# Second mixer: ada sums traced behind a head's maxima, none between heads and out-projection; last feed-forward: prepared weights ahead of the first convolutions

## The chip, the cores and the metric

The kernel runs on one core of a Trainium2 chip. The metric is the device time of one execution in microseconds. The core's engines work side by side, each through its own instructions in order, and wait for one another through semaphores: TensorE (PE; its weight loads are listed as PEld) multiplies matrices, VectorE (DVE) and ScalarE (ACT) do elementwise work and read TensorE's accumulators, GpSimd (POOL) does small elementwise work, and SyncE (SP) issues the DMAs.

## The reference

One step of a two-layer diffusion backbone for two groups of 128 tokens each: a context group and a latent group, which also attends to 128 cached context keys. The model width is 2048, the feed-forward width 5632. Each layer has a mixer and a gated feed-forward, each behind an RMS norm with shift, scale and gate computed from a condition vector:

```python
mod = jax.nn.silu(cond) @ w_ada[l] + b_ada[l]
sh1, sc1, gt1, sh2, sc2, gt2 = jnp.split(mod[:, None, :], 6, axis=-1)
h = rmsnorm(x, g_norm_mix[l]) * (1 + sc1) + sh1
...
x = x + gt1 * m
h = rmsnorm(x, g_norm_ffn[l]) * (1 + sc2) + sh2
x = x + gt2 * conv_ffn(h, w_ffn_up[l], w_ffn_conv[l], b_ffn_conv[l], w_ffn_down[l])
```

The change touches the second layer. Its mixer is differential attention with eight heads of two score halves each:

```python
s = jnp.einsum("bqhjd,bkhjd->bhjqk", qb, k).astype(jnp.float32) * scale
p = jax.nn.softmax(s, axis=-1)
a = (p[:, :, 0] - lam * p[:, :, 1]).astype(v.dtype)
return jnp.einsum("bhqk,bkhd->bqhd", a, v)
...
o = rmsnorm(o, g_sub) * (1.0 - lambda_init)
return o.reshape(b, t, -1) @ w_out, new_ctx
```

Its feed-forward multiplies by w_ffn_up, convolves each feature over three neighbouring positions, and gates:

```python
u = up[:, :-2] * w_conv[0] + up[:, 1:-1] * w_conv[1] + up[:, 2:] * w_conv[2] + b_conv
gate, val = u[..., :D_FF], u[..., D_FF:]
return (jax.nn.silu(gate) * val) @ w_down
```

## The kernel before

**Products.** Features lie on the 128 partitions, the 256 tokens of both groups along the free dimension. A product of one chunk of 128 output features runs through 16 blocks of the weights (`gemm`). Weights and activations are each split into a high part rounded to the fast format and the low remainder, so a block takes three matmuls (high x high, high x low, low x high), and a chunk 48. A weight tile of 1 MB is loaded by SP (`raw`, three buffers), ScalarE rounds it into `wh` and VectorE subtracts that into `wl` (`split`, L240 and L241; `wh` and `wl` have four buffers of half a chunk each). `Weights.ahead` does this for half a chunk before a product asks for it, `first_three` runs the first three chunks of a projection together, with the blocks of the last head (14 and 15) last.

**The order.** The program is traced in Python, and a planner then orders each engine's instructions by a simulated timeline, older ones first among those that are ready. `keep_order` (shortened to `pin` where it is optional) holds an instruction behind the one that was traced just before it on the same engine. In the heads of the second mixer every TensorE instruction is held in this way (`pe.in_turn`).

**The ada work.** The modulation of each sub-layer is computed beside the other work, in three ways. `row_step` does units of it on TensorE. The class `Deep` does six units (`DEEP`) on VectorE: 96 sums (`sums`, L553; each multiplies half a row of weights with the silu of the condition and adds up), whose weight blocks SP loads, one block of two sums at a time, into two buffers (`block`, L550); six further steps load and activate the second half of the condition, and six finish a unit: 108 steps in all. A sum's full product is thrown away into `deep.junk`, which is `o_all` (named hx in the profile) during the heads and `u` (hxc) from the out-projection on. Both the sums and their loads are held in program order. `side_pump`, called by `pump`, takes as many steps as a rate per product says: 2.2 in the heads from the second on, 1.5 in the out-projection.

**The heads.** `project(h)` makes six products per head, two chunks each of query, key and value. Half way through each product its hook `middle` calls `pump`, which advances the earlier head's attention by one stage (`step`), takes side steps, and does a row step; in the last product the hook then also starts this head's `attend`. Its first stage is scores, row maxima (`softmax_parts`, L850 and L851), the negated maxima on GpSimd (L853), exponentials on ScalarE (L858), reciprocals and the combination of the two halves (L1231 to L1237). Later stages transpose the values (`evs`, copied by ScalarE at L1216), transpose and apply the weights, normalise (squares L1260, factor on GpSimd L1264 and L1266, product L1268), transpose back and split the output into `o_all`. After the eighth head `flush` traces its remaining stages.

**The out-projection** follows: `first_three`, then six steps of `Deep` (`AHEAD`), then a loop over 16 chunks with residual (L826), the prepared rows of the next norm (`raw_rows`, L680 and L683) and `pump`.

**The last feed-forward.** `modulated` hands over products already made (`ready`): three in the first layer, four in the second, where no ada unit is left for TensorE, and one further chunk of prepared weights. `conv` takes them one by one: ScalarE scales (L1338), VectorE adds the two neighbours (L1341, L1344). While products are ready its instructions are held in order, and after the one that leaves two products, and the one that leaves one, it calls `W.ahead` for half a chunk.

Of the kernel before, what the change touches and what calls it, by code (L numbers as in the profile page):

```python
# [14 lines left out]
ALU = mybir.AluOpType  # L15
AX = mybir.AxisListType
# [5 lines left out]
T = 128  # L22
# [7 lines left out]
HEAD_SCALE = 128 ** -0.5  # L30
# [23 lines left out]
PEW = {"heads": 1.0, "out0": 1.0, "c": 1.0}  # L54
QUIET = [4, 3, 3]
LATE = 3
AHEAD = 6

EARLY = (2, 5, 8, 11, 13)
WIDER = (32, 16, 8, 4, 2)  # L60
# [22 lines left out]
FLIMIT = {"ab": 0, "ffn0": 12, "c": 12, "ffn1": 16}  # L83

BESIDE = [17, 18, 19]
SIDE = {"in3": 0.6, "heads": 1.05, "out0": 0.9, "c": 2.2, "outc": 1.5}
UW = NT + 2
INV = {2048: 0, 768: 1, 512: 2, 128: 3, 256: 4}

# [2 lines left out]
def step_kernel(ctx: ExitStack, tc: tile.TileContext, A: dict):  # L92
# [419 lines left out]
    def side_pump():  # L512
        side["due"] += side["rate"]
        while side["due"] >= 1.0:
            side["due"] -= 1.0
            side_step()
            deep.step()
# [88 lines left out]
            ada["i"] += 1  # L606
            ada["t"] = 0

    def pump(rows, feats=0.0, until=None):

        until = until or RLIMIT[stage[0]]
        step()
        side_pump()
        ada["due"] += rows
        while ada["due"] >= 0.25:
            if ada["i"] >= until and not later:
                ada["due"] = 0.0
                break
            ada["due"] -= 0.25 if ada["i"] >= until else 0.25 * ada["pew"]
            row_step(until)  # L620
        feat["due"] += feats
        while feat["due"] >= 1.0 and feat["i"] < FLIMIT[stage[0]]:
            feat["due"] -= 1.0
            feature_step()
# [219 lines left out]
        dve.tensor_tensor(out=dst, in0=dst, in1=t[:, :heads], op=ALU.add)  # L844


    def softmax_parts(s, mx, sums, rs, const, p):

        nmx = T_(small, [P, 2], "nmx")
        dve.tensor_reduce(out=mx[:, 0:1], in_=s[:, 0:T], axis=AX.X, op=ALU.max)  # L850
        dve.tensor_reduce(out=mx[:, 1:2], in_=s[:, T:3 * T], axis=AX.X, op=ALU.max)  # L851
        if rs is None:
            pool.tensor_scalar(out=nmx, in0=mx, scalar1=-const, scalar2=None, op0=ALU.mult)  # L853
        else:
            pool.tensor_scalar(out=nmx, in0=mx, scalar1=-1.0, scalar2=None, op0=ALU.mult)
            pool.tensor_tensor(out=nmx, in0=nmx, in1=rs, op=ALU.mult)
        for g, c in ((0, slice(0, T)), (1, slice(T, 3 * T))):
            act.activation(p[:, c], s[:, c], AF.Exp, bias=nmx[:, g:g + 1],  # L858
                           scale=const if rs is None else rs[:, g:g + 1],
                           accum_out=sums[:, g:g + 1])  # L860
# [305 lines left out]
    def mixer_c(cp, hx, W, ready, st):  # L1166
# [4 lines left out]
        def product(rate):  # L1171

            def middle():
                pump(rate)
                while soon:
                    soon.pop(0)()
            return ready.pop(0) if ready else gemm(W.chunk(), xh, xl, between=middle)

        o_all = operand(keep, "hx")
# [38 lines left out]
        def attend(h, q, k, v, evs):  # L1218
            mx = T_(small, [P, 2, 2], "dmx")
            sums = T_(small, [P, 2, 2], "dsums")  # L1220
            pj = []
            for j in range(2):
                s = T_(ppool["att"], [P, 512], "att", bufs=3)
                for g, ks in ((0, slice(0, T)), (1, slice(T, 3 * T))):
                    pe.matmul(s[:, ks], q[:, j, g * T:(g + 1) * T], k[:, j, ks],
                              start=True, stop=True)
                p = T_(cp, [P, 3 * T], f"p{j}", bufs=1)
                softmax_parts(s, mx[:, j], sums[:, j], None, HEAD_SCALE, p)
                pj.append(p)
            rec = T_(small, [P, 2, 2], "drec")  # L1230
            dve.reciprocal(out=rec, in_=sums)  # L1231
            nl = T_(small, [P, 2], "nl")
            dve.tensor_scalar(out=nl, in0=rec[:, 1], scalar1=nlam, scalar2=None, op0=ALU.mult)
            for g, ks in ((0, slice(0, T)), (1, slice(T, 3 * T))):
                dve.tensor_scalar(out=pj[1][:, ks], in0=pj[1][:, ks], scalar1=nl[:, g:g + 1],
                                  scalar2=None, op0=ALU.mult)
                dve.scalar_tensor_tensor(out=pj[0][:, ks], in0=pj[0][:, ks],  # L1237
                                         scalar=rec[:, 0, g:g + 1], in1=pj[1][:, ks],
                                         op0=ALU.mult, op1=ALU.add)
            yield  # L1240
            pt = T_(ppool["att"], [P, 512], "att", bufs=3)
            for i in range(2):
                for g in range(2):
                    pe.transpose(pt[:, g * NT + i * P:g * NT + (i + 1) * P],
                                 evs[:, i, g * T:(g + 1) * T], ident)
            act.copy(v[:, 0], pt[:, 0:NT])
            act.copy(v[:, 2], pt[:, NT:])
            sp.dma_start(out=A["o_diff_v"][:, h], in_=v[:, 0])
            yield
            yield  # L1250
            pT = transposed(cp, pj[0])
            yield
            o = T_(ppool["att"], [P, 512], "att", bufs=3)
            pe.matmul(o[:, 0:NT], pT[:, 0:T], v[:, 0], start=True, stop=True)
            pe.matmul(o[:, NT:], pT[:, T:2 * T], v[:, 1], start=True, stop=False)
            pe.matmul(o[:, NT:], pT[:, 2 * T:], v[:, 2], start=False, stop=True)
            ss = T_(small, [P, 2], "ss")
            on = T_(cp, [P, 2, NT], "on", bufs=1)
            for g in range(2):
                act.activation(on[:, g], o[:, g * NT:(g + 1) * NT], AF.Square,  # L1260
                               accum_out=ss[:, g:g + 1])
            var = T_(small, [P, 2], "var")
            left = (1.0 - LAMBDA_INIT) ** 2
            pool.tensor_scalar(out=var, in0=ss, scalar1=1.0 / (256 * left), scalar2=EPS / left,  # L1264
                               op0=ALU.mult, op1=ALU.add)
            pool.tensor_tensor(out=var, in0=var, in1=C("mhalf")[:, 0:2], op=ALU.pow)  # L1266
            for g in range(2):
                dve.scalar_tensor_tensor(out=on[:, g], in0=o[:, g * NT:(g + 1) * NT],  # L1268
                                         scalar=var[:, g:g + 1], in1=C("gsub"),
                                         op0=ALU.mult, op1=ALU.mult)  # L1270
            yield
            yield
            pt = T_(ppool["att"], [P, 512], "att", bufs=3)
            for i in range(2):
                for g in range(2):
                    pe.transpose(pt[:, i * NT + g * T:i * NT + (g + 1) * T],
                                 on[:, g, i * P:(i + 1) * P], ident)
            src = pt.rearrange("p (i t) -> p i t", i=2)
            split(o_all[:, 2 * h:2 * h + 2, :NT], o_all[:, 2 * h:2 * h + 2, NT:2 * NT], src)
# [11 lines left out]
        oh, ol = (lambda k: o_all[:, k, :NT]), (lambda k: o_all[:, k, NT:2 * NT])  # L1291
        ready = first_three(W, oh, ol, LAST_LATE)
        side["rate"] = SIDE["outc"]
        for _ in range(AHEAD):
            deep.step()
        for c in range(KD):
            fine[0] = c >= KD - QUIET[2]
            residual(ready.pop(0) if ready else gemm(W.chunk(), oh, ol), l, 0, c, st)
# [12 lines left out]
    def ffn(hx, W, ready, turn, l, st):  # L1311
        xh, xl = (lambda k: hx[:, k, :NT]), (lambda k: hx[:, k, NT:2 * NT])
        wider = list(WIDER)

        def product():
            if ready:
                return ready.pop(0)
            if in_order:
                return gemm(W.chunk(), xh, xl, between=in_order.pop(0))
            if wider:  # L1320
                n = NT + wider.pop(0)
                return gemm(W.chunk(), xh, xl, more=lambda k: hx[:, k, :n])
            return gemm(W.chunk(), xh, xl)
# [3 lines left out]
        with tc.tile_pool(name=f"ffn{l}", bufs=1) as fp, banks(f"pffn{l}") as pf:  # L1327
# [5 lines left out]
            def conv(m):  # L1333
                early = bool(ready)
                pin = keep_order if early else lambda i: i
                ps = product()
                y = T_(fp, [P, NT], "cv", bufs=3)
                pin(act.activation(y, ps, AF.Identity, scale=cw[:, 1, m:m + 1], bias=cw[:, 3, m:m + 1]))  # L1338
                y3 = y.rearrange("p (g t) -> p g t", g=2)
                p3 = ps.rearrange("p (g t) -> p g t", g=2)  # L1340
                pin(dve.scalar_tensor_tensor(out=y3[:, :, 1:], in0=p3[:, :, :T - 1],  # L1341
                                             scalar=cw[:, 0, m:m + 1], in1=y3[:, :, 1:],
                                             op0=ALU.mult, op1=ALU.add))
                pin(dve.scalar_tensor_tensor(out=y3[:, :, :T - 1], in0=p3[:, :, 1:],  # L1344
                                             scalar=cw[:, 2, m:m + 1], in1=y3[:, :, :T - 1],
                                             op0=ALU.mult, op1=ALU.add))
                if early and 0 < len(ready) < 3:
                    W.ahead(pin)
                return y

# [233 lines left out]
```

## Time and profile before

| what | us |
|---|---|
| median of three runs (lowest, highest) | 2333.0 (2331.63, 2339.8) |
| the profiled execution's own time | 2332.29 |
| its span, first to last instruction | 2330.5 |
| TensorE busy in the span | 2287.4 |
| VectorE busy | 1873.5 |
| ScalarE busy | 1200.3 |

The stages of the second layer in the span: heads of the mixer until about 1490 us, out-projection from about 1495 to 1598, its feed-forward's first products until about 1620, the rest of that feed-forward and the final norm until the end.

How the rows read. A timeline row has the start in us from the span's beginning, the duration in us, engine, line, operation, what is written and read, how many instructions are merged, and in brackets the engine's idle time before it with what ended that. A row of the chain of waits has start, duration, and the work that the end waited for. A row of windows gives the stretch, its length, then busy time and count for each engine, the clock that TensorE was granted (1.00 is full), the DMA engines' busy share and their rate. Matmuls are pipelined, so a row's duration is longer than the distance from one to the next.

### The profile page before, as it was taken

The numbers are of one execution on the slowest core, as the hardware profiler recorded it, in microseconds if no ns is written. First come the engines' busy times: TensorE is split into PE (matmuls) and PEld (weight loads), VectorE is DVE, ScalarE is ACT, GpSimd is POOL, SyncE is SP. The second block draws the span as 40 slices with busy tenths as digits, with TensorE's granted clock in tenths as the row PEclk, the third lists the DMA queues.
The fourth block names the chain that finished last, engine by engine and source line by source line (L and its number), as shares of the span: only waits on it lengthen the run. The fifth ranks groups of instructions, "written<-read, shape, count | busy, mean of one in ns | idle before, by whom it ended". The sixth has DMA issues, their size and how long they took to land.

```text
span 2330.5 us, 47639 instructions
## 1 busy us (share of the span) xinstructions
PE 2287.4 (98%) x19544; PEld 2187.1 (94%) x19544; DVE 1873.5 (80%) x2920; ACT 1200.3 (52%) x1982; POOL 186.1 (8%) x242
## 2 busy tenths in 40 slices
PE   6999999999999999999999999999999999999998
PEld 4788778999999999999999999999999999999998
DVE  3569767889999999999978878898999965666654
ACT  4245555575553355555575454457655434555543
POOL 0002111210000000001131000014000000000011
PEclk9999999999999999999999999999999999999999
DMA  9888888687777777777788888765777755555553
GB/s 366 346 339 291 314 310 324 231 298 260 260 262 280 300 271 265 260 257 259 290 294 294 296 320 321 280 237 193 255 265 263 261 204 191 192 197 197 188 195 127
DMA packets 102170, 615.05 MB, mean 264 GB/s; under 512 B 11008, under 2 KB 19008, under 8 KB 34752
## 3 DMA queue, kind: packets, MB, share of 16 engines
q1 hardware_dynamic: 101952, 612.01, 71.9%
q8 instruction: 153, 2.51, 0.4%
q14 instruction: 65, 0.53, 0.1%
HBM read 607.22 MB, written 4.75 MB: 263 GB/s over the span
## 4 chain that ended last, share of the span: by engine, by line
PE 91%; DVE 3%; DMA 2%; ACT 1%; issue 1%; POOL 1%; SPq 0%; DVEq 0%; ACTq 0%
PE acc L107 84%; PE ada L107 3%; PE att L107 2%; DVE wl L241 1%; DMA araw<-w_ada 1%; PE att L110 1%; DMA raw<-w_in_ab 1%; ACT wh L240 1%; DMA block<-w_ada 1%; PE misc L107 0%; DVE hx L553 0%; DMA raw<-w_out_c 0%; PE ada L110 0%; POOL dev L790 0%; DVE hxc L553 0%
## 5 line engine op out<-in xcount | busy, mean ns | idle before, releaser
L107 PE MATMUL acc<-hx,wh 128*128 128x256 f32 (+1 forms) x7264 | 1259.1, 278 | 7.8 <-ACT hx L664 4.3
L240 ACT CAST wh<-raw 128x1024 fp32r<-128x1024 f32 (+2 forms) x826 | 795.3, 974 | 912.5 <-PE acc L107 726.8
L107 PEld LDWEIGHTS acc<-hx,wh 128*128 128x128 f32 x7264 | 1101.3, 189 | 38.9 <-issue 15.9
L241 DVE TENSOR_TENSOR wl<-raw,wh 128x1024 fp32r<-128x1024 f32 (+2 forms) x826 | 920.7, 1131 | 254.1 <-ACT wh L240 249.4
L107 PE MATMUL acc<-hx,wl 128*128 128x256 f32 (+1 forms) x3632 | 1007.7, 278 | 4.4 <-DVE wl L241 4.3
L107 PEld LDWEIGHTS acc<-hx,wl 128*128 128x128 f32 x3632 | 685.2, 189 | 6.9 <-DVE wl L241 6.0
L107 PE MATMUL acc<-g,wh 128*128 128x256 f32 x2816 | 478.8, 276 | 0.0
L107 PEld LDWEIGHTS acc<-g,wh 128*128 128x128 f32 x2816 | 423.6, 188 | 0.0
L107 PE MATMUL acc<-g,wl 128*128 128x256 f32 x1408 | 388.0, 276 | 0.0
L456 DVE CUSTOM_DVE_ANT_0 junk<-araw,condb 128x2048 f32<-128x2048 f32 x128 | 294.3, 2300 | 0.0
L107 PE MATMUL acc<-hxc,wh 128*128 128x256 f32 (+1 forms) x1568 | 282.3, 281 | 0.0
L107 PEld LDWEIGHTS acc<-g,wl 128*128 128x128 f32 x1408 | 264.2, 188 | 0.0
L107 PEld LDWEIGHTS acc<-hxc,wh 128*128 128x128 f32 x1568 | 241.2, 189 | 4.5 <-issue 4.2
L107 PE MATMUL acc<-hxc,wl 128*128 128x256 f32 (+1 forms) x784 | 218.2, 278 | 0.0
L203 POOL TENSOR_TENSOR sqacc<-sqacc,sq 128x256 f32<-128x256 f32 x62 | 68.5, 1104 | 1511.5 <-ACT sq L199 1505.4
L107 PEld LDWEIGHTS acc<-hxc,wl 128*128 128x128 f32 x784 | 147.5, 188 | 0.4
L553 DVE CUSTOM_DVE_ANT_0 hx<-block,condb 128x1024 fp32r<-128x1024 f32 x82 | 100.1, 1221 | 18.8 <-DMA block<-w_ada 18.3
L107 PE MATMUL ada<-araw,condw 128*32 128x512 f32 (+1 forms) x672 | 82.6, 591 | 13.7 <-DMA araw<-w_ada 13.6
L1338 ACT ACTIVATE cv<-acc,convw 128x256 f32<-128x256 f32 x169 | 94.4, 559 | 0.0
L826 DVE SCALAR_TENSOR_TENSOR x<-acc,mod,x 128x128 f32<-128x128 f32 x190 | 57.7, 345 | 39.4 <-PE acc L107 39.2
L1344 DVE SCALAR_TENSOR_TENSOR cv<-acc,convw,cv 128x254 f32<-128x254 f32 x169 | 81.0, 479 | 3.1
L1341 DVE SCALAR_TENSOR_TENSOR cv<-acc,convw,cv 128x254 f32<-128x254 f32 x169 | 80.5, 476 | 0.0
(243 smaller groups left out, 1498.7 us busy)
## 6 DMA issues: line engine op xcount, KB each, us to landing
raw<-w_up SPq DMA_DIRECT2D x176, 1024.0 KB, 4.8
araw<-w_ada SPq DMA_DIRECT2D x142, 1024.0 KB, 5.6
raw<-w_down SPq DMA_DIRECT2D x88, 1024.0 KB, 4.8
raw<-w_in_c SPq DMA_DIRECT2D x48, 1024.0 KB, 7.1
block<-w_ada SPq DMA_DIRECT2D x48, 512.0 KB, 6.7
raw<-w_in_ab SPq DMA_DIRECT2D x19, 1024.0 KB, 6.8
raw<-w_out_ab SPq DMA_DIRECT2D x16, 1024.0 KB, 7.0
raw<-w_out_c SPq DMA_DIRECT2D x16, 1024.0 KB, 5.8
```

Source lines behind the costliest of these rows:

```text
L107: return self.placed(nc.tensor.matmul(*a, **kw))
L110: return self.placed(nc.tensor.transpose(*a, **kw))
L203: eng.tensor_tensor(out=st["acc"], in0=st["acc"], in1=sq, op=ALU.add)
L240: pin(act.copy(out_hi, src))
L241: pin(dve.tensor_tensor(out=out_lo, in0=src, in1=out_hi.bitcast(F32), op=ALU.subtract))
L456: keep_order(dve.tensor_tensor_reduce(out=T_(feat["pool"], [P, D], "junk"), in1=feat["row"][:, c], in0=feat["raw"].rearrange("p g n -> p ( ...
L553: keep_order(dve.tensor_tensor_reduce(out=self.junk[:, 14:16, :512], in0=self.raw, in1=self.row[:, c].rearrange("p (g n) -> p g n", g=2), ...
L826: dve.scalar_tensor_tensor(out=x[:, c, s], in0=ps[:, s], scalar=mod[:, l, 3 * which + 2, c, g:g + 1], in1=x[:, c, s], op0=ALU.mult, op1=AL ...
L1338: pin(act.activation(y, ps, AF.Identity, scale=cw[:, 1, m:m + 1], bias=cw[:, 3, m:m + 1]))
L1341: pin(dve.scalar_tensor_tensor(out=y3[:, :, 1:], in0=p3[:, :, :T - 1], scalar=cw[:, 0, m:m + 1], in1=y3[:, :, 1:], op0=ALU.mult, op1=ALU.add))
L1344: pin(dve.scalar_tensor_tensor(out=y3[:, :, :T - 1], in0=p3[:, :, 1:], scalar=cw[:, 2, m:m + 1], in1=y3[:, :, :T - 1], op0=ALU.mult, op1=A ...
```

## The change

Five edits. `AHEAD` and its six steps of `Deep` between `first_three` and the loop go. The out-projection's rate of side steps becomes 2.0 instead of 1.5. In the heads' hook the side steps move from `pump` to the end, behind the start of a head's `attend`. The two maxima of each score half are held in program order. In the second layer's feed-forward the two calls of `W.ahead` move from behind the second and the third convolution to in front of the first and the second; `long` is true where four products are ready.

```diff
-AHEAD = 6
...
-SIDE = {"in3": 0.6, "heads": 1.05, "out0": 0.9, "c": 2.2, "outc": 1.5}
+SIDE = {"in3": 0.6, "heads": 1.05, "out0": 0.9, "c": 2.2, "outc": 2.0}
...
-    def pump(rows, feats=0.0, until=None):
+    def pump(rows, feats=0.0, until=None, beside=True):
 
         until = until or RLIMIT[stage[0]]
         step()
-        side_pump()
+        if beside:
+            side_pump()
...
-    def softmax_parts(s, mx, sums, rs, const, p):
+    def softmax_parts(s, mx, sums, rs, const, p, pin=lambda i: i):
 
         nmx = T_(small, [P, 2], "nmx")
-        dve.tensor_reduce(out=mx[:, 0:1], in_=s[:, 0:T], axis=AX.X, op=ALU.max)
-        dve.tensor_reduce(out=mx[:, 1:2], in_=s[:, T:3 * T], axis=AX.X, op=ALU.max)
+        pin(dve.tensor_reduce(out=mx[:, 0:1], in_=s[:, 0:T], axis=AX.X, op=ALU.max))
+        pin(dve.tensor_reduce(out=mx[:, 1:2], in_=s[:, T:3 * T], axis=AX.X, op=ALU.max))
...
             def middle():
-                pump(rate)
+                pump(rate, beside=False)
                 while soon:
                     soon.pop(0)()
+                side_pump()
...
-                softmax_parts(s, mx[:, j], sums[:, j], None, HEAD_SCALE, p)
+                softmax_parts(s, mx[:, j], sums[:, j], None, HEAD_SCALE, p, keep_order)
...
         side["rate"] = SIDE["outc"]
-        for _ in range(AHEAD):
-            deep.step()
         for c in range(KD):
...
     def ffn(hx, W, ready, turn, l, st):
...
+        long = len(ready) > 3
...
                 pin = keep_order if early else lambda i: i
+                if len(ready) > 4 - 2 * long:
+                    W.ahead(pin)
                 ps = product()
...
-                if early and 0 < len(ready) < 3:
+                if early and ready and not long:
                     W.ahead(pin)
                 return y
```

## The prediction

> **What bounds the kernel now.** I read the page's totals first, then the chain that ended last in order of time, then windows over the two places that the change names, then the timelines there.
>
> ```profile
> span 2330.5 us, 47639 instructions
> PE 2287.4 (98%) x19544; PEld 2187.1 (94%) x19544; DVE 1873.5 (80%) x2920; ACT 1200.3 (52%) x1982; POOL 186.1 (8%) x242
> ```
>
> TensorE is the bound nearly everywhere, so an edit on the other engines can only earn the time in which TensorE waits or runs slowly. The chain leaves TensorE for long in one late place, between the heads of the second mixer and its out-projection, and runs there through VectorE and a load of ada weights:
>
> ```profile
> 1505.17 9.32 DMA block<-w_ada
> 1514.62 1.23 DVE hxc L553
> 1515.89 1.23 DVE hxc L553
> 1517.78 9.96 PE acc L107 x65
> ```
>
> The windows give each stretch: heads, transition, the two halves of the out-projection, the start of the last feed-forward; then two short ones to compare clocks (columns: busy us and count of PE, PEld, DVE, ACT, POOL, granted clock, DMA share, GB/s).
>
> ```profile
> 1213.00:1477.00 264.00, 262.29 (x2203) 250.32 (x2202) 229.04 (x390) 141.54 (x265) 20.87 (x26) 1.00 0.85 307
> ...
> 1511.00:1523.00 12.00, 7.09 (x36) 6.29 (x35) 9.28 (x23) 4.69 (x9) 1.05 (x1) 0.72 0.27 97
> 1523.00:1560.00 37.00, 37.00 (x325) 35.44 (x324) 36.56 (x64) 20.91 (x39) 8.70 (x8) 1.00 0.77 285
> 1560.00:1598.00 38.00, 38.00 (x338) 38.00 (x336) 29.34 (x54) 21.98 (x45) 6.16 (x7) 1.00 0.57 195
> ...
> 1625.00:1632.00 7.00, 5.83 (x48) 5.38 (x47) 6.24 (x12) 6.48 (x11) 0.00 (x0) 1.00 0.76 287
> ```
> ```profile
> 1518.20:1522.40 4.20, 4.20 (x21) 4.20 (x21) 2.86 (x8) 3.34 (x8) 0.00 (x0) 0.50 0.34 122
> 1523.00:1527.00 4.00, 4.00 (x37) 4.00 (x36) 4.00 (x6) 2.78 (x7) 1.70 (x2) 1.00 0.78 262
> ```
>
> TensorE loses about 5 us of 12 in the transition, under 2 of 264 in the heads, 1.2 of 7 at the feed-forward's start, and nothing in the out-projection. What can be won is therefore some 10 us of 2330.
>
> **The transition: no sums between heads and out-projection.** What TensorE, VectorE, ScalarE and GpSimd do there, one fence each:
>
> ```profile
> 1513.30 0.85 PE L110 MATMUL att<-cst,on 128*128 128x128 f32 x4 [1.89 <-DVE on L1268]
> 1514.82 0.61 PE L107 MATMUL acc<-hx,wh 128*128 128x256 f32 x3 [0.68 <-ACT hx L240]
> 1517.78 0.58 PE L107 MATMUL acc<-hx,wh 128*128 128x256 f32 x1 [2.34 <-DVE hx L241]
> ```
> ```profile
> 1510.26 1.22 DVE L553 CUSTOM_DVE_ANT_0 hxc<-block,condb 128x1024 fp32r<-128x1024 f32 x1
> ...
> 1512.67 0.87 DVE L1268 SCALAR_TENSOR_TENSOR on<-att,var,cst 128x256 f32<-128x256 f32 x2
> 1514.62 1.23 DVE L553 CUSTOM_DVE_ANT_0 hxc<-block,condb 128x1024 fp32r<-128x1024 f32 x1 [1.07 <-DMA block<-w_ada]
> ...
> 1517.04 0.69 DVE L241 TENSOR_TENSOR hx<-att,hx 128x512 fp32r<-128x512 f32 x1
> ```
> ```profile
> 1514.19 0.59 ACT L240 CAST hx<-att 128x512 fp32r<-128x512 f32 x1 [4.36 <-PE att L110]
> ```
> ```profile
> 1479.28 0.71 POOL L1266 TENSOR_TENSOR var<-var,cst 128x2 f32<-128x2 f32 x1
> ...
> 1510.48 1.57 POOL L1266 TENSOR_TENSOR var<-var,cst 128x2 f32<-128x2 f32 x1
> ```
>
> The sums that write hxc before the out-projection are the six of AHEAD. The last head's output is late behind the last four of them, two ahead of L1268 and two ahead of the subtraction that writes hx. Without them its hi/lo subtraction starts when ScalarE's cast ends, 1514.19 + 0.59 = 1514.78, not 1517.04: 2.3 us. The norm product L1268 starts when its GpSimd factor is there, 1510.48 + 1.57 = 1512.05, not 1512.67: 0.6. The factor took 0.71 one head earlier, when no sum ran beside it, and 1.57 here beside one: 0.86, an estimate. Together 3.7 of the 4.9 us of waits (1.89 + 0.68 + 2.34). The ends are 2.9 (GpSimd no faster) and 4.9 (the head's chain also starts earlier, since its maxima no longer stand behind a sum).
>
> Behind the wait TensorE ran 21 matmuls in 4.20 us at a granted clock of 0.50; at 1.00 it runs 37 in 4.00. So 4.20 - 21 x 4.00/37 = 1.9 us are lost to the clock. With 1.2 us of waiting left I count all of that as won; the lower end is nothing, since no wait between 0.76 and 4.9 us shows me where the clock falls. The Trainium skill (TensorE: Matmul & The Clock Gate, Why this matters for your kernels) says that a gap of over about 3 us brings the half clock. The trace agrees at 4.9 us; by that rule any end of the row above leaves too short a gap, and the sum keeps 1.9, where the rows alone leave 0 to 1.9.
>
> **What that costs in the out-projection.** The six sums move behind the residuals.
>
> ```profile
> L553 DVE CUSTOM_DVE_ANT_0 hxc<-block,condb 128x1024 fp32r<-128x1024 f32 x14 | 17.6, 1257 | 1.2 <-DMA block<-w_ada 1.1
> ```
>
> Fourteen sums with this form ran: six ahead, eight in the out-projection at 1.5 steps a chunk. Afterwards all fourteen run there, at 2.0 a chunk over eight chunks: 6 x 1.257 = 7.5 us more on VectorE, and three block loads with them. From 1523 to 1560 VectorE is busy 36.56 of 37 us, and yet TensorE never waits; from 1560 on it has 38.00 - 29.34 = 8.7 us free. So the ends are 0 (all of it slides into the later room) and 7.5 (all of it stands before weight splits). The nearest row is the full VectorE without a TensorE wait, so I take a third: 2.5.
>
> **The heads: sums behind the maxima.** Two of the heads' waits are of the kind the change removes; one in full:
>
> ```profile
> 1294.68 1.22 DVE L553 CUSTOM_DVE_ANT_0 hx<-block,condb 128x1024 fp32r<-128x1024 f32 x1
> ...
> 1295.82 0.29 DVE L850 TENSOR_REDUCE dmx<-att 128x1 f32<-128x128 f32 x1
> ```
> ```profile
> 1296.78 0.37 ACT L858 ACTIVATE p<-att,nmx 128x128 f32<-128x128 f32 x1 [3.69 <-POOL nmx L853]
> ...
> 1299.95 0.38 ACT L1216 COPY dev<-acc 128x256 f32<-128x256 f32 x1
> ```
> ```profile
> 1300.39 0.44 PE L110 MATMUL att<-cst,dev 128*128 128x128 f32 x2 [0.76 <-ACT dev L1216]
> ```
> ```profile
> 1340.50 0.44 PE L110 MATMUL att<-cst,dev 128*128 128x128 f32 x2 [0.64 <-ACT dev L1216]
> ```
>
> A sum delays the maxima, the exponentials hold ScalarE 3.69 us, and the copy of the values that TensorE transposes stands behind them. With the maxima over a microsecond earlier ScalarE is free in time: 0.76 + 0.64 = 1.4, of which I take 1.2. The maxima are now held behind the VectorE instruction traced before them, the hi/lo subtraction of the head before, which TensorE has fed by then; that adds no wait. The other end is a loss. Each sum is held behind the VectorE instruction traced just before it; that was work of the step before, and is now the head's last softmax combination (L1237), which waits for both exponentials. Behind the sum stand the next sums and, on SP's queue, the block loads and what follows them there:
>
> ```profile
> 1488.21 9.87 SPq L550 DMA_DIRECT2D block<-w_ada  x2
> 1498.96 0.56 SPq L287 DMA_DIRECT2D raw<-w_out_c  x1
> ```
>
> A block load can thus stand 9.87 us, with a load of weights behind it. About two sums a head, 2.5 us, now fill the time between maxima and combination and will no longer; over seven heads that is 17.6 us, against 264.00 - 229.04 = 35 us in which VectorE is idle in this stretch. I take no loss; all 17.6 on TensorE is the far end. TensorE's order in the heads stays as traced, since the moved calls issue nothing on it there.
>
> **The last feed-forward.**
>
> ```profile
> 1624.07 1.12 ACT L240 CAST wh<-raw 128x512 fp32r<-128x512 f32 x2
> ```
> ```profile
> 1625.13 0.48 DVE L1344 SCALAR_TENSOR_TENSOR cv<-nt,convw,cv 128x254 f32<-128x254 f32 x1
> 1625.53 1.29 DVE L241 TENSOR_TENSOR wl<-raw,wh 128x512 fp32r<-128x512 f32 x2
> ```
> ```profile
> 1626.27 0.38 PE L107 MATMUL acc<-hx,wl 128*128 128x256 f32 x1 [0.53 <-DVE wl L241]
> ...
> 1630.02 0.39 PE L107 MATMUL acc<-hx,wl 128*128 128x256 f32 x1 [0.63 <-DVE wl L241]
> ```
>
> Each half tile is two casts and two subtractions (1.12 and 1.29 us the pair). They move ahead of the first and second convolution, whose two VectorE instructions of 0.48 us come later instead; their results have no reader on TensorE until the down-projection. The weight load itself is long issued in both. Both waits go, 0.53 + 0.63 = 1.2 us; VectorE is busy 6.24 of 7.00 us there, so some of it returns with the next chunk's weights: 0.9 (ends 0 and 1.2). In the first feed-forward the conditions come out as before.
>
> **Sum.** -3.7 - 1.9 + 2.5 - 1.2 - 0.9 = -5.2 us. The profiled execution took 2332.3 us with its span of 2330.5, so 2327.1; the median of the three runs is 0.7 above it, so 2327.8.
>
> **Rivals.** (1) The heads' lumps of sums make weight splits late. For it: the row of the 9.87 us issue, and a VectorE 87% busy. Against it: 35 us idle. It decides once a split stands behind two sums when TensorE needs it. At one sum a head, 7 x 1.257 = 8.8 us in place of the heads' gain: -3.7 - 1.9 + 2.5 + 8.8 - 0.9 = +4.8, 2337.8, slower than before. At its far end of 17.6 it is +13.6, 2346.6. (2) VectorE becomes the bound of the out-projection: its 36.56 of 37 leaves 0.4 us of room, so 7.5 - 0.4 = 7.1 in place of 2.5: 2332.4. (3) Nothing is given back and every end is reached: -4.9 - 1.9 - 1.4 - 1.2 = -9.4, 2323.6; for it, the free 8.7 us. (4) The change doesn't shorten the transition, because another order makes the same chain late (ScalarE's squares stand behind a cast that waits for weights); 1 us or so is left of it: 2332.
>
> **Chances.** Forecast 0.40, rival (1) 0.20 (a third of it beyond +11.7 us), (2) 0.17, (3) 0.15, (4) 0.08. The forecast's own range is 2324 to 2331. The range for the time runs from below (3) to (1): 2321 to 2339. What this measurement can tell from no change is 0.5%, 11.7 us, which is more than all visible waits together (4.9 + 1.9 + 1.4 + 1.2 = 9.4): faster by it 0.04, slower by it 0.08, within it 0.88.
>
> **What would show it.** Right: no L553 between the last combination L1237 and the first residual; a wait before the last head's transposes and behind them of about 1 us together, and a granted clock of 1.00 after it; the two waits for L1216 gone; the first two waits for wl at the feed-forward gone. Wrong: waits of TensorE for wl in the out-projection's chunks 3 to 8 above 5 us (rival 2), waits for wl or hx inside the heads (rival 1), or a transition as long as now (rival 4).

## The result, and the profile after

The changed kernel takes 2324.28 us (median of seven runs, 2321.0 to 2326.12) against 2332.59 for the kernel before on the same chip (2330.81 to 2339.8): a ratio of 0.996, 95% interval 0.9948 to 0.9973. The prediction was 2327.8 within 2321 to 2339, and no difference of over 0.5%. The time lies in that range, but 3.5 us below the point, and nearest to rival (3), in which every wait goes and nothing is given back (2323.6).

Where the 8.9 us between the two spans were won is read from TensorE's timeline. Its order is the same in both kernels but for some matmuls that trade places (above all among the 140 behind the scores of head 7, where the last head's attention stands between the first blocks of the out-projection), so the start of one and the same matmul can be compared. Five of them in the kernel after: scores of heads 0 and 7, the first of the next sub-layer (which reads hxc, behind the out-projection), the last feed-forward's first product, and its first down-projection:

```profile
1213.21 1.47 PE L106 MATMUL att<-dk,dq 128*128 128x128 f32 x8
...
1490.01 1.48 PE L106 MATMUL att<-dk,dq 128*128 128x128 f32 x8
...
1587.84 0.40 PE L106 MATMUL acc<-hxc,wh 128*128 128x258 f32 x2
...
1612.19 0.40 PE L106 MATMUL acc<-hx,wh 128*128 128x256 f32 x2
...
1830.56 0.39 PE L106 MATMUL acc<-g,wh 128*128 128x256 f32 x2
```

The same five in the kernel before:

```profile
1212.86 1.47 PE L107 MATMUL att<-dk,dq 128*128 128x128 f32 x8
...
1490.62 0.39 PE L107 MATMUL att<-dk,dq 128*128 128x128 f32 x2
...
1595.34 0.40 PE L107 MATMUL acc<-hxc,wh 128*128 128x258 f32 x2
...
1619.68 0.40 PE L107 MATMUL acc<-hx,wh 128*128 128x256 f32 x2
...
1839.48 0.39 PE L107 MATMUL acc<-g,wh 128*128 128x256 f32 x2
```

The differences of the distances are the three gains, and every experiment below is read by them. **Heads** (row 1 to 2): 277.76 to 276.80, -1.0. **Transition and out-projection** (2 to 3): 104.72 to 97.83, -6.9. **Feed-forward** (4 to 5): 219.80 to 218.37, -1.4. Between rows 3 and 4 nothing changed (24.34 and 24.35).

The chain of waits in the kernel after no longer leaves TensorE for the sums, only for the last head's cast and subtraction:

```profile
1506.19 4.55 PE acc L106 x40
1510.75 0.45 PE att L109 x4
...
1511.22 0.59 ACT hx L239
...
1511.84 0.70 DVE hx L240
...
1512.58 7.65 PE acc L106 x65
```

Its timelines of TensorE, VectorE, ScalarE and GpSimd at that place (lines 239, 240, 552, 1261, 1267 and 1269 are 240, 241, 553, 1260, 1266 and 1268 of before):

```profile
1510.59 0.60 PE L109 MATMUL att<-cst,on 128*128 128x128 f32 x4
1511.86 1.11 PE L106 MATMUL acc<-hx,wh 128*128 128x256 f32 x4 [0.68 <-ACT hx L239]
```
```profile
1500.90 1.22 DVE L552 CUSTOM_DVE_ANT_0 hx<-block,condb 128x1024 fp32r<-128x1024 f32 x1
...
1508.17 0.88 DVE L1269 SCALAR_TENSOR_TENSOR on<-att,var,cst 128x256 f32<-128x256 f32 x2 [2.65 <-POOL var L1267]
1511.84 0.69 DVE L240 TENSOR_TENSOR hx<-att,hx 128x512 fp32r<-128x512 f32 x1 [2.79 <-ACT hx L239]
...
1517.88 1.22 DVE L552 CUSTOM_DVE_ANT_0 hxc<-block,condb 128x1024 fp32r<-128x1024 f32 x1
```
```profile
1506.23 0.38 ACT L1261 ACTIVATE on<-att 128x256 f32<-128x256 f32 x1 [1.97 <-PE att L106]
```
```profile
1507.43 0.71 POOL L1267 TENSOR_TENSOR var<-var,cst 128x2 f32<-128x2 f32 x1
```

No sum runs between 1502.2 and 1517.8, VectorE waits for its inputs, the factor takes 0.71 us, and of the three waits only the 0.68 us for the cast is left. The predicted sign, no sum at all between the last combination and the first residual, didn't come to the letter: two of the heads' sums run behind the combination, the later one at 1500.90, but both end 6 us ahead of the norm product. The windows after (heads, transition, the two halves of the out-projection, start of the feed-forward):

```profile
1213.00:1476.40 263.40, 262.89 (x2206) 251.20 (x2205) 228.95 (x387) 141.19 (x265) 15.53 (x26) 1.00 0.83 302
1508.50:1515.00 6.50, 5.72 (x48) 5.28 (x48) 2.76 (x8) 2.17 (x4) 0.00 (x0) 1.00 0.22 91
1515.00:1552.50 37.50, 37.50 (x330) 35.94 (x329) 37.50 (x68) 22.07 (x40) 9.13 (x7) 1.00 0.77 285
1552.50:1590.50 38.00, 38.00 (x338) 38.00 (x336) 35.90 (x69) 22.76 (x49) 7.54 (x7) 1.00 0.65 233
1617.50:1624.50 7.00, 7.00 (x62) 7.00 (x61) 6.72 (x11) 6.30 (x10) 0.00 (x0) 1.00 0.96 390
```

The clock is 1.00 behind the transition. VectorE is now busy 37.50 of 37.50 us in the first half of the out-projection and 35.90 of 38.00 in the second (29.34 before), and TensorE never waits in either. The feed-forward's start has no idle time left.

### The profile page after: what moved, and what is told of

Same layout as the page of the kernel before. It is cut to its first block, busy times and chain, and to the rows that moved or that the text cites. A ratio compares the mean times of both kernels' runs of the same rounds, so it can differ in the third digit from the quotient of the medians.

```text
span 2321.6 us, 47643 instructions
## 1 busy us (share of the span) xinstructions
PE 2280.7 (98%) x19544; PEld 2182.1 (94%) x19544; DVE 1873.0 (81%) x2920; ACT 1200.1 (52%) x1982; POOL 182.5 (8%) x242
## 4 chain that ended last, share of the span: by engine, by line
PE 95%; DMA 2%; DVE 2%; ACT 1%; issue 0%; SPq 0%; POOL 0%; DVEq 0%; ACTq 0%
PE acc L106 87%; PE ada L106 3%; PE att L106 2%; PE att L109 1%; DMA raw<-w_in_ab 1%; DMA araw<-w_ada 1%; DVE wl L240 1%; DMA block<-w_ada 1%; PE misc L106 0%; PE ada L109 0%; ACT wh L239 0%; DVE x L1448 0%; DVE nt L654 0%; DVE aacc L484 0%; DVE ql L930 0%
```

## The experiments

The theory to be tested: the six sums are what lengthens the transition; in the out-projection they cost nothing, since VectorE works on weights that TensorE needs only later; the gains of the three parts add up. The rivals: the sums cost TensorE time wherever VectorE is full; the gain comes from elsewhere.

**Each part alone.** First the transition's edit:

```diff
-AHEAD = 6
+AHEAD = 0
-SIDE = {..., "outc": 1.5}
+SIDE = {..., "outc": 2.0}
```

> The kernel before with no steps between heads and out-projection and the rate of 2.0, nothing else. Theory (the sums stood ahead of the last head's output): from the scores of the last head to the end of the out-projection TensorE gains 2.9 to 5.6 us (2.9 from the two places ahead of the norm product and the subtraction, 0.9 if the norm factor on GpSimd is quicker, 1.9 from the clock), the heads and the feed-forward nothing. Rival (the gain of that stretch comes from the maxima of the last head, which are earlier in the heads' part of the change): under 2 us here.

2328.34 us (ten runs) against 2332.95: 0.9986 (0.9975 to 0.9998). Its transition had the same single wait as the changed kernel, and yet the stretch to the end of the out-projection became only 4.4 us shorter instead of 6.9. The 2.5 us are no wait. The windows over the same 636 matmuls of the out-projection, in this kernel and then in the changed one:

```profile
1515.00:1589.60 74.60, 74.60 (x636) 73.03 (x636) 70.76 (x130) 42.34 (x84) 16.02 (x14) 1.00 0.71 258
```
```profile
1515.50:1587.80 72.30, 72.30 (x636) 70.74 (x636) 70.49 (x130) 42.28 (x84) 16.67 (x14) 1.00 0.73 265
```

TensorE is busy throughout in both, at a granted clock of 1.00, but takes 2.3 us longer. In the starts of single matmuls two spacings show, 0.1134 and 0.1178 us; 568 of 639 in the changed kernel kept the first, 572 of 639 here the second (the expectations below count 16 more to each). Whether that belongs to the edit was tested by a second run of both:

> The transition's edit alone, once more. In its first profile 588 of the out-projection's 639 matmuls ran at the slow spacing of 0.1178 us, which is 2.6 us more than at the fast one, and from the scores of head 7 to the end of the out-projection it won 4.4 us. Theory A (the spacing belongs to the kernel): slow again, 4.4 us again, and the edit is worth 4.4 us. Theory B (the spacing is a phase of the run): in another phase the same stretch wins 6.9 us, as the whole change does. By either, no wait of TensorE for wl inside the out-projection.

> The changed kernel once more, to see what a second profile of the same instructions shows. The matmuls of 256 columns run at one of two spacings, 0.1134 us or 0.1178 us from start to start, and keep one of them for tens of microseconds: in the first profile of this kernel 584 of the out-projection's 639 run at the fast one. Theory A (the spacing belongs to the kernel, through where its buffers lie): again about 584 fast and the same landmarks within 0.5 us from the scores of head 0 to the end. Theory B (the spacing is a phase that a run falls into): another pattern, and the out-projection up to 2.6 us longer. Time by both 2322 to 2327 us, ratio to the kernel before 0.995 to 0.998.

In its second profile the same kernel with the transition's edit ran the fast spacing:

```profile
1523.46:1595.76 72.30, 72.30 (x636) 70.74 (x636) 70.49 (x130) 42.26 (x84) 16.48 (x14) 1.00 0.73 265
```

Its transition and out-projection took 97.89 us, 6.8 less than before, as much as the whole change's 97.83. The spacing is thus a matter of the run, not of this edit, and the edit is worth 6.8 us when it is alike. The changed kernel again: 2323.76 us (six runs) against 2334.70, ratio 0.995 (0.9934 to 0.9965), with 97.83 us and 568 matmuls at the fast spacing once more. The edit alone had a median of 2327.96, 0.9975 (0.9961 to 0.9989).

The heads' edits alone (the changed kernel with the six steps where they were, the old rate and the old feed-forward):

```diff
+        for _ in range(6):
+            deep.step()
-SIDE = {..., "outc": 2.0}
+SIDE = {..., "outc": 1.5}
```

> The changed kernel with the six steps put back between heads and out-projection, the rate of 1.5 and the old places in the feed-forward, so that only the heads' part is left. Theory: the scores of the last head come 0.9 to 1.0 us earlier than before, as in the changed kernel; from there to the end of the out-projection at most 1 us more is gained, since the four sums still stand ahead of the last head's output. Rival (the last head's earlier maxima make the gain): 4 us or more there.

One run, 2335.22 us, whose first stages were 5 us longer than in most others although nothing is edited there. The heads took 276.89 us, 0.9 less than before, and the transition kept part of its wait:

```profile
1516.69 1.23 DVE L552 CUSTOM_DVE_ANT_0 hxc<-block,condb 128x1024 fp32r<-128x1024 f32 x1 [0.57 <-DMA block<-w_ada]
...
1517.84 0.69 DVE L240 TENSOR_TENSOR hx<-att,hx 128x512 fp32r<-128x512 f32 x1
```
```profile
1517.07 0.62 PE L106 MATMUL acc<-hx,wh 128*128 128x256 f32 x3 [0.68 <-ACT hx L239]
1518.58 0.39 PE L106 MATMUL acc<-hx,wh 128*128 128x256 f32 x1 [0.89 <-DVE hx L240]
```
```profile
1518.60:1522.40 3.80, 3.80 (x22) 3.80 (x23) 3.80 (x11) 2.99 (x6) 0.00 (x0) 0.65 0.47 163
```

The fifth sum waits 0.57 us for its block and so stands right ahead of the last head's subtraction; TensorE waits 0.89 us for that, and the clock falls.

The expected 1 us at most was wrong. From the scores of head 7 to the first matmul behind that subtraction it took 27.16 us before, 23.36 here and 22.57 in the changed kernel: with all six sums still there, the heads' edits alone win 3.8 of the 4.6 us. To the end of the out-projection it is 102.54 us, 2.2 less than before, though 566 of the 639 matmuls ran at the slow spacing, which makes the last 584 of them 2.1 us longer (68.91 against 66.78). The wait of 1.89 us ahead of the transposes is gone as in the changed kernel, and that of 2.34 us is down to 0.89. That it is the last head's earlier maxima, as the rival says, isn't shown: these edits also put TensorE's matmuls behind those scores in the changed kernel's order, and move the loads on SP's queue.

The feed-forward's edit alone, on the kernel before:

```diff
+                if len(ready) > 4 - 2 * long:
+                    W.ahead(pin)
-                if early and 0 < len(ready) < 3:
+                if early and ready and not long:
```

> The kernel before with the two half tiles ahead of the first two convolutions of the last feed-forward, nothing else. Theory: all is as before up to the feed-forward, and its down-projection begins 1.2 to 1.5 us earlier, both waits for the low parts gone. Rival (the waits move to the next chunk): under 0.5 us.

One run, 2329.16 us. From the feed-forward's first product to its first down-projection 218.37 us, 1.4 less than before: the whole gain of this part. The transition, in which not an instruction differs from before, came out 1.3 us shorter, so one profile can't resolve less than that there as long as the sums' loads decide. The first matmul behind the last head's output came at 25.57 us instead of 27.16: measured against this profile, the heads' edits alone won 2.2 us there and not 3.8, still more than expected.

So the parts don't add up as the theory has it. The transition's 6.8, the feed-forward's 1.4 and the heads' 0.9 inside the heads make 9.1 of the 9.3 of all together, but only because what the heads' edits win in the transition is left out. Two edits win the same time there: either of them alone takes much of it, and together they win no more than the transition's edit by itself. The six sums lengthen the transition by 6.8 us in the order of before, but with the heads' edits in place only by 0.8 us of waiting and what the slower clock behind it costs.

**How many of the six steps cost.** Two and four of them put back into the changed kernel, at its rate of 2.0:

```diff
         side["rate"] = SIDE["outc"]
+        for _ in range(4):
+            deep.step()
```

> The changed kernel with two of the six steps put back between heads and out-projection. Theory (a step costs only where it stands ahead of the last head's norm product or output, and VectorE is idle 2.65 us ahead of that product): both fit into idle time, the stretch from the last head's scores to the end of the out-projection is the same within 0.5 us. Rival (each step there costs its own time): 2.5 us longer.

> The changed kernel with four of the six steps put back. Theory: the third and fourth stand ahead of the norm product or the output and cost 1 to 2.5 us; the waits together stay under 3 us and the granted clock behind them stays 1.00. Rival (the clock falls after shorter waits too): the clock behind the waits is 0.50 for some matmuls, and the stretch is 3 to 4.5 us longer.

2323.6 and 2323.89 us, one run each; the stretch took 97.84 us in both, as in the changed kernel. The expected 1 to 2.5 us of the four steps didn't come. VectorE's timeline with four:

```profile
1507.19 1.23 DVE L552 CUSTOM_DVE_ANT_0 hxc<-block,condb 128x1024 fp32r<-128x1024 f32 x1 [1.19 <-DMA block<-w_ada]
...
1508.35 0.87 DVE L1269 SCALAR_TENSOR_TENSOR on<-att,var,cst 128x256 f32<-128x256 f32 x2
1509.14 1.22 DVE L552 CUSTOM_DVE_ANT_0 hxc<-block,condb 128x1024 fp32r<-128x1024 f32 x1
...
1511.18 0.69 DVE L240 TENSOR_TENSOR hx<-att,hx 128x512 fp32r<-128x512 f32 x1 [0.82 <-ACT hx L239]
```

The third ends as the norm product can start, and the fourth ends 0.82 us before the cast that the subtraction waits for anyway. Four sums fit into the gaps of the last head's chain; it is the last two, behind one more block load, that don't. This holds with the heads' edits in place; fewer than six were not tried on the order of before.

**What a full VectorE costs in the out-projection.** Extra VectorE work of a sum's size, one (9.8 us together) or two per chunk in the first eight chunks:

```diff
         for c in range(KD):
+            for _ in range(1 if c < 8 else 0):
+                keep_order(dve.tensor_tensor_reduce(..., accum_out=T_(small, [P, 2], "extra")[:, 0:1]))
```

> The changed kernel with one more VectorE instruction of a sum's size, kept in order, behind each of the first eight chunks of the out-projection (its product is thrown away): 8 x 1.22 = 9.8 us more on VectorE. Theory (the six moved sums cost nothing because VectorE still had room, of which some 2 us are left in 75 us): TensorE waits for low parts and the out-projection is 4 to 8 us longer. Rival (the planner lets such work slide behind the weights wherever it is, as far as the next norm's preparation): under 1 us.

> The same with two more behind each of the first eight chunks: 19.5 us more on VectorE. Theory: 13 to 18 us longer. Rival: under 3 us.

2359.24 and 2370.95 us. Of the 36 and 48 us that their spans lost, a large part is not the mechanism under test: the slow spacing ran through much of their first layer, their heads and their last down-projection, and summed over all starts costs an estimated 23 us more than in the changed kernel (some 5200 more matmuls at it, 0.0044 us each). One group of the pages shows it (busy us, mean ns of one), with one extra sum a chunk and then in the changed kernel:

```profile
L106 PE MATMUL acc<-g,wh 128*128 128x256 f32 x2816 | 497.5, 279 | 0.0
```
```profile
L106 PE MATMUL acc<-g,wh 128*128 128x256 f32 x2816 | 478.8, 276 | 0.0
```

The out-projection stretch stayed within 0.6 us of the changed kernel's in both; the next norm's preparation lost 6.2 and 30 us. The 4 to 8 and 13 to 18 us that were expected inside the out-projection didn't come. As these kernels have one more small buffer, the test was repeated without a new one, by running every sum of the out-projection twice into the same places:

```diff
+            for _ in range(deep.twice):
+                keep_order(dve.tensor_tensor_reduce(..., accum_out=out))
```

> Every sum of the out-projection is run twice into the same places, with no new buffer: 14 more VectorE instructions of 1.25 us, 17.5 us. Theory A (sums slide behind the weight splits, which run ahead of TensorE): the stretch from the scores of head 7 to the end of the out-projection is at most 1 us longer than in the changed kernel, no wait for wl over 1 us in it, and what is lost (5 to 13 us) is lost in the norm's preparation behind it, where the residual's statistics come late. Rival (2) of the prediction (VectorE is the bound of the out-projection): TensorE waits for wl inside it, by 10 to 17 us together.

2348.53 us, one run. The out-projection, then the next norm's preparation in three pieces:

```profile
1515.12:1587.70 72.58, 72.58 (x636) 70.91 (x636) 72.58 (x130) 39.99 (x78) 16.02 (x13) 1.00 0.67 241
...
1590.00:1600.70 10.70, 6.31 (x31) 6.05 (x29) 10.43 (x19) 2.77 (x6) 2.03 (x2) 0.70 0.60 211
1600.70:1616.00 15.30, 0.54 (x3) 0.25 (x2) 13.16 (x32) 10.73 (x31) 12.93 (x18) 0.61 0.00 0
1616.00:1630.00 14.00, 14.00 (x95) 13.83 (x96) 9.18 (x17) 7.41 (x18) 4.24 (x7) 0.80 0.28 95
```
```profile
1594.94 0.59 PE L106 MATMUL att<-cst,sq 128*128 128x1 f32 x2 [4.15 <-ACT sq L198]
...
1615.86 1.04 PE L106 MATMUL acc<-hxc,wh 128*128 128x258 f32 x2 [14.76 <-ACT hxc L708]
```

VectorE is busy for all of 72.58 us, and TensorE doesn't wait once in the out-projection; the stretch from the scores of head 7 took 98.12 us (+0.3). The added 17.5 us aren't in it: VectorE runs 130 instructions in this window as in the changed kernel's, 2.1 us more of work, and 8 of the 28 sums start behind it. Behind it 25.2 us are lost, more than the 5 to 13 expected: two waits of 18.9 us together, and the slower clock behind each. The first ends with squares that stand behind the last residual. The second ends with a row of the next norm (L708) that reads what the sums themselves make; VectorE's timeline has the last of them and the last step of that unit:

```profile
1609.45 1.21 DVE L556 CUSTOM_DVE_ANT_0 hxc<-block,condb 128x1024 fp32r<-128x1024 f32 x1
...
1614.74 0.15 DVE L564 TENSOR_TENSOR mod<-mod,cst 128x8 f32<-128x8 f32 x1
```

So the sums do slide, until their own results and the last residuals are due. Rival (2) has the wrong place; its kind of cost exists one stage later, from the point where the sums don't end before the last chunks.

**The held maxima.** The changed kernel without them:

```diff
-                softmax_parts(s, mx[:, j], sums[:, j], None, HEAD_SCALE, p, keep_order)
+                softmax_parts(s, mx[:, j], sums[:, j], None, HEAD_SCALE, p)
```

> The changed kernel without holding the maxima in program order. Theory: it is the order of tracing that puts the sums behind the maxima, and holding them adds nothing: the same within 0.5 us at every stage. Rival (the planner lets the maxima slip without it): the wait for the copied values at the third head's place is back, 0.6 to 0.8 us, or the transition is 1 us longer.

> The change without holding the heads' maxima in their traced place, timed. In one profile its heads took 1.2 us less than the changed kernel's, with no wait left for the copy of the values. If that is the edit: 1.2 us again in the heads, and a median about 1 us under that of the changed kernel run beside it, too little for the interval of one of them to exclude the other. If it is the variation of a run: the heads as in the changed kernel within 0.5 us.

2324.35 us in one run, then 2323.14 (median of six, 2322.13 to 2325.66; ratio 0.9949, 0.9932 to 0.9967). In the two profiles the heads took 275.55 and 275.73 us, against 276.80 and 276.57 in the two of the changed kernel: neither the same, as the first expectation's theory said, nor the wait back, as its rival did, but less. The second profile's window over the heads, and the wait left with the pins in the changed kernel's first profile:

```profile
1213.00:1476.00 263.00, 263.00 (x2213) 251.07 (x2215) 229.44 (x387) 141.83 (x268) 15.48 (x26) 1.00 0.83 301
```
```profile
1339.90 0.44 PE L109 MATMUL att<-cst,dev 128*128 128x128 f32 x2 [0.51 <-ACT dev L1217]
```

The planner, left free, removes the last such wait too, so the moved side steps win the heads' time and holding the maxima gives about 1 us of it back. In the whole time that is 0.6 us between two medians whose runs overlap: it shows in the traces, and the times can't confirm it.

## Why the prediction was right, and where its sizes were off

**The out-projection: the term that failed is the +2.5.** It measured nothing: 636 matmuls in 72.30 us without a wait. I took a third of 7.5 because VectorE was full. Being full is no price by itself: VectorE there works on weights for later chunks, and the sums ran until 1564.6 us, over 20 us ahead of the stage's end. Right was the row beside it, the free time in the second half: the 7.5 us fit in. But it was nearer to a price than the waits show. Pair every subtraction that writes wl, in order, with the first matmul that reads what it wrote. In the out-projection's loop, behind its first tile, the subtraction ends at least 4.1 us ahead of that matmul in the kernel before, 2.0 with four steps put back, 1.2 with two, and 0.5 in the changed kernel, just behind the last sum:

```profile
1564.58 1.21 DVE L240 TENSOR_TENSOR wl<-raw,wh 128x1024 fp32r<-128x1024 f32 x1
```
```profile
1566.31 0.28 PE L106 MATMUL acc<-hx,wl 128*128 128x256 f32 x1
```

With the sums run twice the lead falls to 0.05 us and still no wait comes, as other work goes behind instead. That fits the planner, which sets the order by its simulated timeline; an order that can't give way wasn't tried.

**The transition: -3.7 measured -4.8, the clock's -1.9 measured -2.1.** To the sixth matmul behind the transposes the distance from the scores of head 7 went from 27.76 to 22.91 us, the rest of the 6.9 is won behind it. (The same instructions in the feed-forward's experiment took 1.3 us less than before, so 6.9 is the upper of two values.) The steps that I named all came: no sum just ahead of the norm product or of the subtraction, the factor 0.71 instead of 1.57 us. What I had only as a reason for the far end, a chain that starts earlier, is ahead of them, and it isn't the maxima's doing: with the transition's edit alone they stood where they had been, 4.95 us behind the scores, and the squares started 1.2 us earlier. In the kernel before, the cast that stands before the squares on ScalarE was late:

```profile
1508.04 1.05 ACT L240 CAST wh<-raw 128x1024 fp32r<-128x1024 f32 x1 [3.92 <-DMA raw<-w_out_c]
1508.99 0.38 ACT L1260 ACTIVATE on<-att 128x256 f32<-128x256 f32 x1
```

It waited 3.92 us for weights; in the kernel after the squares wait for TensorE alone and start at 1506.23, 2.2 us earlier against the scores of head 7. I had seen this cast and made it an argument for rival (4). That the block loads between heads and out-projection made those weights late fits, but isn't shown: with the heads' edits alone, or with four steps, the loads were there and the squares didn't wait for the cast. With the transition's edit alone the cast still waited 1.83 us in the second profile, and the stretch was won all the same. What the prediction missed is that the heads' edits win in this place too: it gave them a term in the heads alone. It also read 4.9 us of waiting as one gap that brings the slower clock; they are three waits, the longest 2.34 us.

**The feed-forward: -0.9 measured -1.4**, above the end of 1.2 that I gave. That end was the sum of the two waits as their rows print them. A row's wait counts from the modelled end of the matmul before, 0.28 us behind its start, while the next one starts 0.1134 us behind it in a full stream. Each printed wait is thus 0.17 us too short: 0.53 + 0.63 + 2 x 0.17 = 1.5. The same holds for the transition's waits.

**The heads: -1.2 measured -1.0.** That is one pair of profiles; against the four with the old order, 277.0 to 279.6 us, it is 0.2 to 2.8. The first of the two waits went, the second shrank from 0.64 to 0.51 us. The lumps of sums that rival (1) feared made no split late; the sums waited for their blocks less than before, 5.1 us where it had been 18.3.

**The rivals.** (3) was nearest: of its -9.4 the profiles show -9.3. It wasn't right term by term: the heads stayed below their end (1.0 of 1.4), the feed-forward went above its own (1.4 over 1.2), and what made it the nearest is the out-projection, in which nothing was given back. (1) and (4) fell with the windows above, (2) with the leads and the doubled sums.

## What to carry to other kernels

An engine that is busy all the time in a stretch has not run out of room: look how far its work is ahead of the one that reads it, and at which later point it must be empty; extra work is free up to there and costs beyond (here 25.2 us for 17.5 added). Two edits that each win on their own may win the same time: test each alone and compare the sum in each stage, not only in the whole. Work that fills gaps belongs ahead of or behind a chain that all engines wait for, and the tightest part of that chain sets how much fits: here four sums did and six didn't, behind the moved heads' sums. Measure a gain as the distance between two fixed matmuls in one trace rather than by printed waits or total times, since a run varies by more than a change like this.

## What the runs showed of the hardware

**Two spacings at one granted clock.** Matmuls of 256 columns follow one another in 0.1134 or 0.1178 us, both at a clock of 1.00. A run keeps one of them through nearly a whole out-projection, and the same kernel had the slow one in one profile and the fast one in another: 2.3 us in 72.3. In the changed kernel's out-projection it changes only where ada matmuls stand between. In the two kernels with the extra buffer it was slow for nearly all matmuls of the heads and for half of those from 700 us to the heads and of the last down-projection. What sets it stays open.

**The clock falls after less than one long wait.** With the heads' edits alone the granted clock went to 0.65 in the window behind two waits of 0.68 and 0.89 us, 1.5 us apart; behind the 0.68 us alone it stayed at 1.00, as it did in the heads behind single waits of 1.16 and 1.07 us (the second profile of the transition's edit). The Trainium skill (TensorE: Matmul & The Clock Gate, Why this matters for your kernels) gives a gap of over about 3 us; this trace shows the fall with no gap near that. Nor does the kernel before have one, with 2.34 us as its longest wait there, so the prediction was wrong to count its trace as agreement.

**Unequal spread.** The runs of the kernel before lie between 2327.3 and 2340.7 us, and those with the transition's edit alone between 2323.6 and 2336.3; those of the changed kernel between 2321.0 and 2326.1. The heads with the old order took 277.0 to 279.6 us in four profiles, with the new order and held maxima 276.6 to 276.9 in six (the two with extra VectorE work and the slow spacing aside). That is a part of the spread; the rest wasn't tried.
